# Moved value rows of a causal convolution: copied inside the chip instead of through DRAM

## The chip, the cores and the metric

The kernel runs on one core of one Trainium2 chip. The metric is the device time of one execution in microseconds (us), median of several runs. The core has five engines, each with its own instruction stream in order: TensorE (PE, matrix products), VectorE (DVE), ScalarE (ACT), GpSimd (POOL) and SyncE (SP). Data move between DRAM and the on-chip memory (128 partitions), and inside the on-chip memory too, by DMA. A DMA is issued by SP, ACT or POOL and runs on up to 16 DMA engines, beside the five engines. All numbers are float32.

## The reference, cut to what matters

One decoder layer on 256 tokens of 2048 channels. After a normalisation, one wide input projection makes q, k, v, z, two small gate inputs, a pooling input and two more gates. A causal convolution of width 4 runs over the 256 tokens of q, k and v, each channel by itself:

```python
def causal_dwconv(x, w):
    width = w.shape[0]
    seq = x.shape[1]
    xp = jnp.pad(x, ((0, 0), (width - 1, 0), (0, 0)))
    y = xp[:, 0:seq] * w[0]
    for j in range(1, width):
        y = y + xp[:, j:j + seq] * w[j]
    return y
...
qkv = jax.nn.silu(causal_dwconv(jnp.concatenate([q, k, v], axis=-1), conv_qkv_w[l]))
```

So a token's value row needs the row itself and the rows one, two and three tokens before it, each times a weight for each channel; before the first token there are zeros. The rest (the gated delta rule over the convolved q, k, v, the pooling mixer, the gates, the output projection, and a gated MLP of 5632 channels) is the same in both kernels.

## The kernel before, in words

**Work of PE.** The large products stream their weights. A tile of weights has 256 rows of the contraction and 512 columns, 512 KB, and is named `raw` when it has landed. To keep float32 accuracy it is split in two: ACT casts it to `whi` (L317, `begin`), DVE subtracts and gets `wlo` (L328), and PE does three products for each (L365 to L367, in `gemm_a`): 12 matmuls of 512 columns for each tile of weights. There are four buffers of `raw` and three pairs `whi`, `wlo`; `weights()` keeps the split two tiles ahead of the one in use. A load of `raw` is issued by SP (L223, `load_part`) as soon as the split has freed its buffer.

**Order of the input projection.** The columns are done in four groups `g` of 512 (four heads each). In each group PE projects k, q, v, the pooling input, a gate, z (with the small pooling product) and the other gate, eight tiles of weights each (`for g in range(4)`, L1095). A projection ends in a PSUM tile; `evict` (L776) scales it by the row's normaliser on ACT into the on-chip tile `e`, which has the one buffer `ev`. For k, q and v the tokens lie along the partitions: `e` is 128 partitions by 2 by 512, token `t * 128 + p` at partition `p`, half `t`.

**k and q** are turned by PE so that tokens lie along the free dimension, and their convolution is three shifted multiply-adds on DVE (`conv_silu`, L825); its result tile `y` has the tag `cy`, two buffers.

**v** stays with tokens along the partitions, where a shift by a token is a shift by a partition, which no DVE instruction does. So:
- before the projection starts, DVE sets a small tile `zr` to zero, and four DMAs issued by ACT write three zero rows ahead of each group's place in a DRAM tensor `vrow` (L768 to L774);
- after the eviction of v, SP writes `e` to `vrow` (L1122);
- in `v_moved` (L800), DVE multiplies `e` by the last tap (L802), and SP loads three copies from `vrow`, moved by one, two and three tokens (L807): each a tile `m` of 128 partitions by 2 by 512;
- in `v_conv` (L810), DVE multiplies each `m` by its tap (L816) and adds it to the sum (L817), in the order one, two, three tokens; ACT does the tanh of the silu (L820).

The homes of the three tiles `m`: the copies by one and two use the two buffers of `cy` (which k's and q's convolution results have held before), the copy by three uses the single buffer `mv` (which `zr` held at first).

**What sets the order.** Each `dma_start`, product and sum is placed on its engine's stream by a planner when the program is built; it follows the dependences, the order of the code, and a model of the durations. `tc.issue_after(x)` sets an instruction behind another. Work that is to run during the next projection is put in the list `later`, and `gemm_a` calls it when it comes to its second tile of weights (L358 to L360): `v_moved` of a group thus stands in the projection of the pooling input, just behind v's. `side()` (L368) advances the delta rule of the group by a step for every half tile of weights. In `v_conv`, the product with copy `n` is set behind the split number `splits_of[g] + n`, and three further in group 0 (L815).

The next eviction, that of the pooling input, writes the single buffer `ev` again.

Of the kernel before, what the change touches and what calls it, by code (L numbers as in the profile page):

```python
# [8 lines left out]
F32 = mybir.dt.float32  # L9
# [5 lines left out]
P = 128  # L15
S = 256
# [19 lines left out]
def kernel(  # L36
# [20 lines left out]
    nc = tc.nc  # L57
# [5 lines left out]
    dpool = ctx.enter_context(tc.tile_pool(name="dram", bufs=2, space=bass.MemoryType.DRAM))  # L63
# [5 lines left out]
    def nm(s):  # L69
        cnt[0] += 1  # L70
        return f"{s}_{cnt[0]}"
# [282 lines left out]
    def gemm_a(lh, ll, nk, steps=None, ps=None):  # L354

        ps = pm() if ps is None else ps
        for c in range(nk // 2) if steps is None else steps:
            if c == 1:  # L358
                while later:
                    later.pop(0)()  # L360
            hi, lo = weights()
            for kk in range(2):
                k = 2 * c + kk
                for t in range(2):
                    mm(ps[:, t, :], lh(k, t), hi[:, kk, :], start=(k == 0), stop=False)  # L365
                    mm(ps[:, t, :], ll(k, t), hi[:, kk, :], start=False, stop=False)  # L366
                    mm(ps[:, t, :], lh(k, t), lo[:, kk, :], start=False, stop=(k == nk - 1))  # L367
                side()  # L368
        return ps
# [65 lines left out]
    mp = mix.__enter__()  # L435
# [46 lines left out]
    def parts_x(pts):  # L482
        for k, pt in pts:
            high, low = (both(xhl, k)[:, n, :] for n in range(2))
            hi = nc.scalar.activation(high, pt, AF.Copy, scale=nmw[:, k : k + 1])
            lo = nc.vector.scalar_tensor_tensor(low, pt, nmw[:, k : k + 1], high.bitcast(F32),
                                                op0=ALU.mult, op1=ALU.subtract)
        return hi.ins, lo.ins
# [28 lines left out]
    with tc.manual_schedule(engines={mybir.EngineType.PE, mybir.EngineType.DVE, mybir.EngineType.Activation}):  # L517
# [21 lines left out]
        for c in range(4):  # L539
            if c:  # L540
                tile_k0(2 * c)
            if c < 3:
# [3 lines left out]
                last_act, last_dve = parts_x(pts[2:])  # L546
# [219 lines left out]


    SH = 3  # L768
    vrow = dpool.tile([4, SH + S, 512], F32, tag="vrow", bufs=1, name="vrow")
    zr = mp.tile([P, 2, 512], F32, tag="mv", name="zr")  # L770
    nc.vector.memset(zr[:SH, 0, :], 0.0)
    for g in range(4):
        with tc.issue_after(last_act):
            nc.scalar.dma_start(vrow[g, 0:SH, :], zr[:SH, 0, :])  # L774

    def evict(ps, by=None):  # L776

        by = rs1 if by is None else by
        e = mp.tile([P, 2, 512], F32, tag="ev", bufs=1, name=nm("ev"))
        for t in range(2):  # L780
            nc.scalar.activation(e[:, t, :], ps[:, t, :], AF.Copy, scale=by[:, t : t + 1])
        return e
# [17 lines left out]
    def v_moved(e, g, vt):  # L800

        nc.vector.tensor_tensor(vt, e, taps_of[g][3], op=ALU.mult)  # L802
        moved_of[g] = []
        splits_of[g] = len(splits)
        for j in (1, 2, 3):
            m = mp.tile([P, 2, 512], F32, name=nm("mv"), **(dict(tag="cy", bufs=2) if j < 3 else dict(tag="mv")))
            nc.sync.dma_start(m, vrow[g, SH - j : SH - j + S, :].rearrange("(t p) d -> p t d", p=P))  # L807
            moved_of[g].append(m)

    def v_conv(g, vt):  # L810
# [284 lines left out]
    for g in range(4):  # L1095
        kq = mp.tile([P, 4, 2, S], F32, tag="kq", bufs=1, name=nm("kq"))
        for kind, dst in ((1, kq[:, :, 0, :]), (0, kq[:, :, 1, :])):
            ps = ps_k0 if kind == 1 and g == 0 else gemm_a(xh, xl, KD)
            e = evict(ps)
# [19 lines left out]

            later.append(after_k)  # L1120
        e = evict(gemm_a(xh, xl, KD), rsh)
        nc.sync.dma_start(vrow[g, SH : SH + S, :].rearrange("(t p) d -> p t d", p=P), e)  # L1122
        later.append(lambda e=e, g=g, vt2=vt2: v_moved(e, g, vt2))


# [3 lines left out]
        e = evict(ps) if g == 3 else evict(ps, rsh)  # L1129
# [608 lines left out]
```

## Time and profile before

| | |
|---|---|
| time, median of 3 runs | 1537.4 us (1536.69 to 1538.38) |
| the profiled execution | 1538.56 us, of which the span from the first to the last instruction is 1536.8 us |
| granted clock of TensorE | 0.998 of full speed |
| moved rows, DMA issues | 4 writes of 512 KB, 12 loads of 512 KB, 4 zero writes of 6 KB |
| evictions of v | begin at 86.65, 263.74, 441.12 and 619.69 us |

How to read the views that follow. On the page, a line of an engine gives busy time, share of the span and number of instructions; a queue line gives packets, MB and the time of its packets as a share of 16 engines' span; q1 is SP's queue and q10 ACT's. A group of instructions gives the line of the code, the engine, the operation, the tiles it writes and reads, the count, busy time, the mean in ns, and the idle time before it with what ended it. A row of the waits says who waited for whom: total us, how often, the longest. A row of the timeline gives the start and the length in us, the engine, the line, the tiles, the count; the bracket has the idle time before it and what ended it. SPq is a DMA issued by SP. A row of the stretches gives the stretch, its length, busy time and count of PE, the weight load, DVE, ACT and POOL, then the granted clock, the busy share of the DMA engines, and GB/s. Rows of DMA issues give the count, the size of each and, where known, the median us from issue to landing.

### The profile page before, as it was taken

The page shows a single profiled execution, that of the slowest core. Times are in us where ns is not written, and L with a number is a line of the kernel's source. Part 1 is how long each engine was busy: PE and PEld are TensorE (multiplying, and loading weights), DVE is VectorE, ACT ScalarE, POOL GpSimd, SP SyncE. Part 2 cuts the span into 40 slices and gives each one's busy share as a digit, 9 for nine tenths or more (in the row PEclk, how much of TensorE's full clock was granted, in tenths as well). Part 3 has the DMA queues.
Part 4 walks back from the last instruction along what each step waited for, and adds up shares of the span by engine and source line. Part 5 has one row for each costly group of instructions (what it writes and reads, how often), then busy time and mean ns, then how long its engine had stood idle before and what let it go on. Part 6 is the DMA issues. An engine that isn't in the chain of part 4 may idle for free. (4 is left out here: it accounts for less than half of the span.)

```text
span 1536.8 us, 20233 instructions
## 1 busy us (share of the span) xinstructions
PE 1524.3 (99%) x7290; PEld 1255.4 (82%) x7290; DVE 1268.3 (83%) x1793; ACT 853.1 (56%) x1070; POOL 80.9 (5%) x105
## 2 busy tenths in 40 slices
PE   9999999999999999999999999999999999999997
PEld 8887888787878888788888888788888888888876
DVE  6788859896589858887567899999999886889896
ACT  6455446454455445454455666666666665555553
POOL 1010002000100000000000000000000011010200
PEclk9999999999999999999999999999999999999999
DMA  8776757776576766776588556656457478566662
GB/s 276 209 229 198 203 165 207 218 216 185 148 250 201 208 169 194 231 195 186 171 263 305 179 178 219 219 206 206 154 165 243 127 238 266 172 223 207 235 201 98
DMA packets 166515, 313.62 MB, mean 204 GB/s; under 512 B 19554, under 2 KB 23426, under 8 KB 166286
## 3 DMA queue, kind: packets, MB, share of 16 engines
q1 hardware_dynamic: 157280, 283.17, 59.2%
q0 software_dynamic: 7344, 27.27, 5.5%
q10 hardware_dynamic: 1790, 1.89, 0.4%
q8 instruction: 57, 0.93, 0.3%
q14 instruction: 44, 0.36, 0.1%
HBM read 303.33 MB, written 8.95 MB: 203 GB/s over the span
## 5 line engine op out<-in xcount | busy, mean ns | idle before, releaser
L317 ACT CAST whi<-raw 128x1024 fp32r<-128x1024 f32 x420 | 441.2, 1052 | 427.1 <-PE psm L366 270.0
L328 DVE TENSOR_TENSOR wlo<-raw,whi 128x1024 fp32r<-128x1024 f32 x418 | 507.7, 1220 | 146.0 <-ACT whi L317 140.2
L317 ACT CAST whi<-quad 128x1024 fp32r<-128x1024 f32 x182 | 190.5, 1053 | 136.8 <-PE psg L1418 43.5
L328 DVE TENSOR_TENSOR wlo<-quad,whi 128x1024 fp32r<-128x1024 f32 x182 | 220.0, 1219 | 30.0 <-ACT whi L317 29.4
L367 PE MATMUL psm<-wlo,xhl 128*128 128x512 f32 x432 | 169.5, 393 | 1.3 <-DVE wlo L328 1.2
L365 PE MATMUL psm<-whi,xhl 128*128 128x512 f32 x432 | 169.0, 391 | 0.0
L366 PE MATMUL psm<-whi,xhl 128*128 128x512 f32 x432 | 168.6, 390 | 0.0
L1418 PE MATMUL psg<-whi,fhl 128*128 128x512 f32 x504 | 127.2, 390 | 0.0
L1418 PEld LDWEIGHTS psg<-whi,fhl 128*128 128x128 f32 x504 | 94.5, 188 | 19.6
L367 PEld LDWEIGHTS psm<-wlo,xhl 128*128 128x128 f32 x432 | 81.1, 188 | 18.8 <-DVE wlo L328 2.2
L366 PEld LDWEIGHTS psm<-whi,xhl 128*128 128x128 f32 x432 | 81.1, 188 | 16.8
L365 PEld LDWEIGHTS psm<-whi,xhl 128*128 128x128 f32 x432 | 81.1, 188 | 16.7
L244 DVE TENSOR_TENSOR quad<-quad,quad 128x1024 f32<-128x1024 f32 x72 | 87.6, 1216 | 0.0
L1418 PE MATMUL psg<-wlo,fhl 128*128 128x512 f32 x252 | 69.9, 389 | 0.0
L1418 PE MATMUL psg<-whi,ups 128*128 128x512 f32 x216 | 58.9, 394 | 0.0
L1418 PEld LDWEIGHTS psg<-wlo,fhl 128*128 128x128 f32 x252 | 47.3, 188 | 9.9
L1403 PE MATMUL psm<-whi,hhi 128*128 128x512 f32 (+1 forms) x140 | 54.5, 389 | 0.1
L1403 PE MATMUL psm<-whi,hlo 128*128 128x512 f32 (+1 forms) x140 | 54.1, 386 | 0.0
L1403 PE MATMUL psm<-wlo,hhi 128*128 128x512 f32 (+1 forms) x140 | 54.0, 387 | 0.0
L365 PE MATMUL psm<-whi,mhi 128*128 128x512 f32 x128 | 50.8, 397 | 0.0
L367 PE MATMUL psm<-wlo,mhi 128*128 128x512 f32 x128 | 50.0, 390 | 0.0
L366 PE MATMUL psm<-whi,mlo 128*128 128x512 f32 x128 | 49.9, 390 | 0.0
(435 smaller groups left out, 2953.7 us busy)
## 6 DMA issues: line engine op xcount, KB each, us to landing
raw<-in_w_in_dram SPq DMA_DIRECT2D x224, 512.0 KB, 4.3
raw<-in_w_up_dram SPq DMA_DIRECT2D x104, 512.0 KB, 4.8
quad<-in_w_up_dram SPq DMA_DIRECT2D x72, 512.0 KB, 5.0
raw<-in_w_down_dram SPq DMA_DIRECT2D x56, 512.0 KB, 5.1
raw<-in_w_out_dram SPq DMA_DIRECT2D x32, 512.0 KB, 4.2
quad<-in_w_down_dram POOLq DMA_DIRECT2D x32, 512.0 KB, 5.3
mv<-vrow SPq DMA_DIRECT2D x12, 512.0 KB, 4.8
taps<-in_conv_qkv_w_dram SPq DMA_DIRECT2D x16, 256.0 KB, 6.6
```

Of the source, the lines that this page charges most:

```text
L244: nc.vector.tensor_tensor(out_, plus_, minus_, op=ALU.subtract)
L317: last_cast[0] = nc.scalar.copy(hi, raw).ins
L328: last_split[0] = nc.vector.tensor_tensor(lo, raw, hi.bitcast(F32), op=ALU.subtract).ins
L365: mm(ps[:, t, :], lh(k, t), hi[:, kk, :], start=(k == 0), stop=False)
L366: mm(ps[:, t, :], ll(k, t), hi[:, kk, :], start=False, stop=False)
L367: mm(ps[:, t, :], lh(k, t), lo[:, kk, :], start=False, stop=(k == nk - 1))
L1403: mm(ps[:, cs], lhs(kk), part_[:, kk, cs], start=(first and kk == 0 and n == 0), stop=(last and kk == 1 and n == 2), skip_group_check=shared)
L1418: mm(ps, lhs(kk), w[n][:, kk], start=(first and n == 0 and kk == 0 and lhs is high), stop=False, skip_group_check=True)
```

## The change

DRAM is left out of the move. The tensor `vrow`, the zero rows and the write of `e` go. Each moved tile is now made of three pieces: POOL sets its first `j` rows of half 0 to zero; a DMA issued by ACT copies the last `j` partitions of half 0 of `e` to the first `j` partitions of half 1; a DMA issued by SP copies the first `128 - j` partitions of `e`, both halves, to the partitions from `j` on. Homes: the copy by one token now uses `mv`, those by two and three use `cy`. The products and sums on them are as before.

```diff
-    vrow = dpool.tile([4, SH + S, 512], F32, tag="vrow", bufs=1, name="vrow")
-    zr = mp.tile([P, 2, 512], F32, tag="mv", name="zr")
-    nc.vector.memset(zr[:SH, 0, :], 0.0)
-    for g in range(4):
-        with tc.issue_after(last_act):
-            nc.scalar.dma_start(vrow[g, 0:SH, :], zr[:SH, 0, :])
...
         for j in (1, 2, 3):
-            m = mp.tile([P, 2, 512], F32, name=nm("mv"), **(dict(tag="cy", bufs=2) if j < 3 else dict(tag="mv")))
-            nc.sync.dma_start(m, vrow[g, SH - j : SH - j + S, :].rearrange("(t p) d -> p t d", p=P))
+            m = mp.tile([P, 2, 512], F32, name=nm("mv"), **(dict(tag="cy", bufs=2) if j > 1 else dict(tag="mv")))
+            nc.gpsimd.memset(m[0:j, 0, :], 0.0)
+            nc.scalar.dma_start(m[0:j, 1, :], e[P - j :, 0, :])
+            nc.sync.dma_start(m[j:], e[: P - j])
             moved_of[g].append(m)
...
         e = evict(gemm_a(xh, xl, KD), rsh)
-        nc.sync.dma_start(vrow[g, SH : SH + S, :].rearrange("(t p) d -> p t d", p=P), e)
         later.append(lambda e=e, g=g, vt2=vt2: v_moved(e, g, vt2))
```

## The prediction

> **What bounds the kernel now.** I read the page first (its time by engine, its DMA queues, its groups of instructions), then the waits, then the stretches around the four moves.
>
> ```profile
> span 1536.8 us, 20233 instructions
> PE 1524.3 (99%) x7290; PEld 1255.4 (82%) x7290; DVE 1268.3 (83%) x1793; ACT 853.1 (56%) x1070; POOL 80.9 (5%) x105
> ...
> q1 hardware_dynamic: 157280, 283.17, 59.2%
> ...
> q10 hardware_dynamic: 1790, 1.89, 0.4%
> ...
> L317 ACT CAST whi<-raw 128x1024 fp32r<-128x1024 f32 x420 | 441.2, 1052 | 427.1 <-PE psm L366 270.0
> ```
>
> TensorE is busy for 1524.3 of 1536.8 us: whatever the change saves elsewhere can come out only where PE stands still. The waits of the engines, and the busy time of each engine in the stretch behind a V eviction (group 0 and group 2; the first pair of numbers is the length and PE's busy time), say how little that is around the moved rows:
>
> ```profile
> DVE mv L816 <- DMA mv<-vrow: 11.2, 4, 4.5
> ```
>
> ```profile
> 86.00:112.00 26.00, 26.00 (x112) 20.86 (x112) 22.68 (x35) 12.74 (x15) 1.93 (x1) 1.00 0.83 253
> 441.00:467.00 26.00, 24.80 (x107) 19.54 (x106) 20.78 (x33) 10.52 (x13) 2.08 (x1) 1.00 0.74 241
> ```
>
> DVE waits 11.2 us in all for the moved rows, once in each of the four groups. PE feels one of the four, the longest (4.5 us): in group 2 it is busy for 24.80 of 26 us, in group 0 for all 26. So the round trip through DRAM costs this execution about 1.2 us, and a perfect change returns 1.2 us.
>
> **What is removed, and at what price.** Four writes of 512 KB (L1122), four small zero writes issued by ACT and one memset go; twelve loads of 512 KB (L807) become copies inside the chip.
>
> ```profile
> 88.72 0.47 SPq L1122 DMA_DIRECT2D vrow<-ev  x1
> 91.75 0.37 SPq L223 DMA_DIRECT2D raw<-in_w_in_dram  x1
> 94.67 0.88 SPq L807 DMA_DIRECT2D mv<-vrow  x2
> ```
>
> ```profile
> 90.51 1.22 DVE L328 TENSOR_TENSOR wlo<-raw,whi 128x1024 fp32r<-128x1024 f32 x1
> ...
> 93.31 1.23 DVE L846 SCALAR_TENSOR_TENSOR kq<-th,cy 128x1024 f32<-128x1024 f32 x1
> ...
> 96.21 1.23 DVE L328 TENSOR_TENSOR wlo<-raw,whi 128x1024 fp32r<-128x1024 f32 x1 [0.54 <-ACT whi L317]
> 99.69 1.23 DVE L816 TENSOR_TENSOR mv<-mv,taps 128x1024 f32<-128x1024 f32 x1 [2.25 <-DMA mv<-vrow]
> ```
>
> ```profile
> 103.18 0.39 PE L365 MATMUL psm<-whi,xhl 128*128 128x512 f32 x1
> ...
> 105.90 0.39 PE L365 MATMUL psm<-whi,xhl 128*128 128x512 f32 x1
> ```
>
> ```profile
> DMA to landing us min/median/max: 4.3/4.8/5.0
> ```
>
> In group 0 SP issues the write at 88.72 and the loads only from 94.67, when the write has landed. Straight copies can go at about 88.7, 6.0 us sooner. Were each as quick as the loads (4.8 us), DVE's 2.25 us stall would go; the next thing late is nothing on PE. This part is worth 0 to -1.2 us over the whole run, and I take -1.2.
>
> **What is added: how many DMA engines serve a copy.** The loads land 128 partitions. The copies land 127, 126 and 125 (`m[j:]`). The profile has no such transfer on SP's queue, but ACT's queue q10 has some with odd counts, and its packets can be counted from the list of issues:
>
> ```profile
> psb<-in_pool_scale_dram ACTq DMA_DIRECT2D x4, 256.0 KB
> ...
> out_dram<-xt ACTq DMA_DIRECT2D x2, 256.0 KB
> ...
> cqrows<-in_conv_qkv_w_dram ACTq DMA_DIRECT2D x1, 96.0 KB, 2.9
> cfrows<-in_conv_ffn_w_dram ACTq DMA_DIRECT2D x1, 66.0 KB
> gwb<-in_gdn_norm_w_dram ACTq DMA_DIRECT2D x1, 64.0 KB, 3.8
> vrow<-zr ACTq DMA_DIRECT2D x4, 6.0 KB
> vrows<-in_conv_ffn_b_dram ACTq DMA_DIRECT2D x1, 22.0 KB
> nmrows<-in_norm_mix_w_dram ACTq DMA_DIRECT2D x1, 8.0 KB
> alb<-in_a_log_dram ACTq DMA_DIRECT2D x1, 8.0 KB
> dtb<-in_dt_bias_dram ACTq DMA_DIRECT2D x1, 8.0 KB
> vrows<-in_norm_ffn_w_dram ACTq DMA_DIRECT2D x1, 8.0 KB, 3.4
> ```
>
> By the shapes in the code these 18 transfers consist of 512 + 256 + 192 + 132 + 128 + 12 + 44 + 16 + 128 + 128 + 16 = 1564 contiguous pieces. The queue shows 1790 packets, 226 more. If every transfer ended with one packet on each of 16 engines there would be 288 more. The 62 that are missing are what the odd shapes leave out if a transfer runs on the largest number of engines, 16 at most, that divides its rows: 3 rows on 3 engines (4 times 13 missing), 66 and 44 rows on 11 each (twice 5): 52 + 10 = 62. SP's queue, where all counts are multiples of 16, fits with 16 each. So I take the rule that the rows give: 127 rows are prime and go on **one** engine, 126 on 14, 125 on 5.
>
> The Trainium skill says the same of transfers issued from SP and ACT, with 127 partitions on one engine as an example (page "DMA: Bandwidth & Descriptors", section "Why a DMA increments its semaphore by 16 and not by 1"); the 226 agree, but no run so far shows 127 rows.
>
> **The price of one engine.** I take the time of a packet from a stretch in which the engines were nearly full, 30.61 to 32.95 us:
>
> ```profile
> q1 hardware_dynamic: 397, 0.78, 95.1%
> ```
>
> 0.951 x 16 x 2340 ns / 397 = 89.7 ns for a packet of 2 KB, so 179 ns for a row of 4 KB. (All of q1 on the page gives 92.6 ns.) The copy by one row: 127 x 179 = 22.8 us on one engine. By two: 126/14 = 9 rows, 1.6 us. By three: 125/5 = 25 rows, 4.5 us. A weight load: 256 packets over 16 engines, 1.4 us on each. An engine that all three use is held for 28.9 us, and it serves a sixteenth of every weight load behind them on SP's queue.
>
> **What waits for it, in group 0.** A tile of weights feeds 12 matmuls, 2.72 us (103.18 to 105.90, both first matmuls of a tile). Four raw buffers: the split that ends at 91.73 frees the one for the tile that PE begins at 105.90, and its load goes out at 91.75, behind the copies. It has to be there by 105.90 - 1.05 (cast) - 1.22 (split) = 103.6. A load of 4.8 us is 7.1 us early; that is the cover. Of those 4.8 us 1.4 are packets, so 3.4 are start and queue. With the copies out at 88.7 the first lands at 88.7 + 3.4 + 22.8 = 114.9. The load behind it and behind the copy by two lands at 114.9 + 1.6 + 1.4 = 117.9, its tile is ready at 120.2, and PE stands for 14.3 us. The copy by three waits for its new home until the q convolution has been read (93.31 + 1.23 = 94.5), as the loads did, so it may stand ahead of the next load: that one lands at 117.9 + 4.5 + 1.4 = 123.8 and is ready at 126.1, 3.2 us after PE wants it. Upper reading 17.5 us. The start may overlap with what is in flight, which takes up to 3.4 us off: lower reading 10.9 us.
>
> DVE gives nearly the same by its own way: the product L816 stands behind the split of 96.21, and the splits behind it wait for the first copy until 114.9. The split of that same tile would end at about 114.9 + 1.2 + 1.2 = 117.3, against PE's 105.90: 11.4 us. The two waits run side by side, and the longer counts. I take **15 us a group**, inside 10.9 to 17.5. In the other groups the product may stand three splits earlier (the code sets it behind a split three tiles sooner there), and PE would run dry sooner but also wait for the same landing. Four groups: 60 us.
>
> **The small pieces** (12 memsets on POOL, 12 ACT copies of 2 to 6 KB).
>
> ```profile
> L774 ACTq DMA_DIRECT2D vrow<-zr x4: 238/265/283, 28.2 to 30.2; - x4
> ```
>
> Three issues of 0.27 us are 0.8 us of ACT, busy for 12.74 of 26 us in that stretch; POOL has one instruction there, 1.93 us. On ACT the third waits for the same home as SP's copy by three (94.5); a cast behind it could lose 0 to 1.4 us. Three memsets on POOL, each at most as long as that instruction, are at most 5.8 us, in an engine that is idle for 24. I take 0; if POOL or ACT held the copies back as well, the bound is 3 us a group, 12 in all. The next eviction reuses `ev` and now waits on ACT until the copies have read it, at 114.9 + 1.6 + 4.5 = 121.0; PE ends that projection at 120.2 + 2.7 = 122.9, so nothing is added.
>
> **The sum.** -1.2 + 60 = +59 us, rounded: 1596 us span against 1536.8. The profiled execution took 1538.56 us beside a median of 1537.4 (1536.69 to 1538.38), so I put it on the median: 1596.5.
>
> **The rivals.**
> - *The copies are spread over all 16 engines after all.* Then each lands in about 4.8 us, DVE's four waits go, and PE gets back its 1.2 us: 1536.2 us, not slower. It decides at one point: a first copy that lands in under about 12 us from its issue (4.8 plus the 7.1 of cover) stalls no load. For it: all twelve loads of 128 rows landed in 4.3 to 5.0. Against it: the 62 missing packets. The same section of the Trainium skill tells of direct copies issued from GpSimd that put 127 rows on 16 engines; by that 1536.2 would come out, but these go from SP. Chance 0.08.
> - *The cover is larger than I count*: two more weight loads slip ahead of the copies, so that the first delayed tile is needed 2 x 2.72 us later, and the start overlaps wholly. 15 - 5.4 - 3.4 = 6.2 us a group, +24 in all: 1561 us. For it: SP's order is planned anew, and SP issued one load between the write and the loads of rows. Against it: a raw buffer comes free only every 2.72 us, and the copies need nothing that is later than 88.7. Chance 0.05.
> - *The waits chain*: memset, ACT's piece and SP's copy one behind the other, or one engine slower still when it reads and writes inside the chip. A first copy 1.75 times as long, 40 us for 22.8, adds 17 a group: +128, about 1665 us. Chance 0.07.
> - The forecast, 0.80.
>
> The range has my readings and bounds: 4 x 8.2 - 1.2 (10.9 less one load slipped ahead, 2.7) = +31, 1568, to 4 x 20.5 + 12 - 1.2 = +93, 1630 (17.5, and about one tile, 3 us, more where the product stands three splits earlier; 12 for the small pieces). It leaves out 0.20. A measurement of this kernel tells about 0.2%, 3 us, from no change. Even spread gives "same" nearly always: same 0.06, faster 0.02, slower 0.92.
>
> **What would show it.** Right: `mv<-ev` copies that land 20 us or more after their issue; DVE waiting some 15 us a group for them at the product; weight loads in the same 25 us that land in 15 to 25 us; PE busy for some 11 of the 26 us behind each V eviction, and as full as before elsewhere. On q1 four groups lose 4 x 272 packets each (the write and three loads, 256 + 16) and get 128 + 140 + 130 (rows and one packet for each engine): 157280 - 2760 = 154520, where an even spread over 16 would leave 154632. Wrong: copies that land in 5 us, or PE full in those stretches. If they are slow but PE stands for under 8 us a group, the cover was undercounted; if PE loses time outside the four stretches, a wait on ACT or POOL that I put at 0 is the cause.

## The result and the profile after

The changed kernel takes 1626.93 us (median of 4 runs, 1624.64 to 1628.39) beside 1537.55 us for the kernel before: a ratio of 1.058, 95% interval 1.0567 to 1.0593. The forecast was 1596.5 us, range 1568 to 1630. The loss has the sign, the place and the cause that were forecast, and is half as large again: +89.4 us against +59.

The page after; its lines answer to those of the page before (span, time by engine, queues):

```profile
span 1625.3 us, 20278 instructions
PE 1537.4 (95%) x7290; PEld 1260.8 (78%) x7290; DVE 1267.2 (78%) x1792; ACT 853.0 (52%) x1070; POOL 84.1 (5%) x117
...
q1 hardware_dynamic: 154520, 280.98, 55.8%
```

DVE and ACT do the same work as before. The span is 88.5 us longer, and PE's busy time 13.1 us: the rest, 75.4 us, is PE standing still. SP's queue has 154520 packets, which is the number worked out for copies on 1, 14 and 5 engines; an even spread would have left 154632.

The waits after, with total, times and longest:

```profile
ACT whi L317 <- DMA raw<-in_w_in_dram: 99.2, 14, 22.8
DVE mv L812 <- DMA mv<-ev: 94.6, 7, 22.0
...
PE psm L367 <- DVE wlo L328: 58.3, 11, 18.3
```

The second row was 11.2 us in 4 times before, and the first was small:

```profile
ACT whi L317 <- DMA raw<-in_w_in_dram: 7.4, 4, 2.5
```

ACT waits for weight loads, DVE for the moved rows, PE for DVE's splits.

The 26 us behind the four V evictions (from 87, 282, 480 and 679 us):

```profile
87.00:113.00 26.00, 19.46 (x83) 15.03 (x81) 10.57 (x14) 6.69 (x8) 0.52 (x1) 0.97 0.45 131
282.00:308.00 26.00, 15.61 (x66) 11.93 (x64) 5.91 (x5) 6.44 (x8) 0.52 (x1) 0.90 0.49 137
480.00:506.00 26.00, 10.93 (x49) 8.72 (x47) 5.44 (x8) 5.79 (x7) 0.00 (x0) 0.77 0.32 97
679.00:705.00 26.00, 11.01 (x49) 8.79 (x47) 5.63 (x7) 5.60 (x8) 0.52 (x1) 0.81 0.33 98
```

Where PE was full, it now works for 11 to 19 of 26 us, and the DMA engines are busy for a third to a half (share next to last) instead of about three quarters and more. For part of the time one of them works alone: from 500 to 505 us SP's queue has 31 packets of 4 KB, one row each, and they take 6.2% of 16 engines' time, which is one engine of 16.

Group 0 in order of time, first SP's issues, then DVE, then ACT:

```profile
84.22 5.23 SPq L223 DMA_DIRECT2D raw<-in_w_in_dram  x3
89.96 2.48 SPq L803 DMA_DIRECT2D mv<-ev  x2
93.04 12.32 SPq L223 DMA_DIRECT2D raw<-in_w_in_dram  x2
```

```profile
97.20 1.23 DVE L328 TENSOR_TENSOR wlo<-raw,whi 128x1024 fp32r<-128x1024 f32 x1 [0.79 <-ACT whi L317]
117.34 1.23 DVE L812 TENSOR_TENSOR mv<-mv,taps 128x1024 f32<-128x1024 f32 x1 [18.92 <-DMA mv<-ev]
```

```profile
119.99 1.04 ACT L317 CAST whi<-raw 128x1024 fp32r<-128x1024 f32 x1 [22.82 <-DMA raw<-in_w_in_dram]
```

The first copy goes out at 89.96, and DVE can use it at 117.34: 27.4 us. In groups 1, 2 and 3 the same distance is 26.1, 25.2 and 24.4 us. The weight load issued at 93.04, behind the copies, is there for the cast at 119.99, 27 us later; such a load took 4.3 us before (median).

The holes of PE that are longer than 2 us, all of them (five rows of PE's timeline; the bracket is the hole):

```profile
121.09 0.79 PE L365 MATMUL psm<-whi,xhl 128*128 128x512 f32 x1 [14.63 <-ACT whi L317]
...
313.13 0.79 PE L367 MATMUL psm<-wlo,xhl2b 128*128 128x512 f32 x1 [15.53 <-DVE wlo L328]
...
320.27 0.80 PE L367 MATMUL psm<-wlo,xhl 128*128 128x512 f32 x1 [2.60 <-DVE wlo L328]
...
509.28 0.80 PE L367 MATMUL psm<-wlo,xhl2a 128*128 128x512 f32 x1 [18.34 <-DVE wlo L328]
...
707.88 0.79 PE L367 MATMUL psm<-wlo,xhl2a 128*128 128x512 f32 x1 [17.88 <-DVE wlo L328]
```

Together 69.0 us, one large hole in each group. In group 0 a late weight load ends the large hole, in the others the splits behind the product that waited.

### The profile page after: what moved, and what is told of

It is laid out like the page before. It is cut to its first block, busy times and chain, and to the rows that moved or that the text cites. A ratio compares the mean times of both kernels' runs of the same rounds, so it can differ in the third digit from the quotient of the medians.

```text
span 1625.3 us, 20278 instructions
## 1 busy us (share of the span) xinstructions
PE 1537.4 (95%) x7290; PEld 1260.8 (78%) x7290; DVE 1267.2 (78%) x1792; ACT 853.0 (52%) x1070; POOL 84.1 (5%) x117
## 3 DMA queue, kind: packets, MB, share of 16 engines
q1 hardware_dynamic: 154520, 280.98, 55.8%
q0 software_dynamic: 7344, 27.27, 5.1%
q10 hardware_dynamic: 1934, 1.91, 0.4%
## 5 line engine op out<-in xcount | busy, mean ns | idle before, releaser
L365 PE MATMUL psm<-whi,xhl 128*128 128x512 f32 x432 | 170.5, 395 | 14.6 <-ACT whi L317 14.6
L812 DVE TENSOR_TENSOR mv<-mv,taps 128x1024 f32<-128x1024 f32 x12 | 14.7, 1223 | 94.6 <-DMA mv<-ev 94.6
L367 PE MATMUL psm<-wlo,xhl2a 128*128 128x512 f32 x108 | 44.6, 413 | 36.2 <-DVE wlo L328 36.2
L367 PE MATMUL psm<-wlo,xhl2b 128*128 128x512 f32 x108 | 43.7, 405 | 16.3 <-DVE wlo L328 16.3
```

Source lines behind the costliest of these rows:

```text
L812: nc.vector.tensor_tensor(m, m, taps_of[g][j], op=ALU.mult)
```

## The experiments

**The theory:** a DMA with 127 rows runs on one DMA engine and one with 125 rows on five; DVE's product waits for the copy, and the weight loads behind it on SP's queue wait for their sixteenth. **Rivals:** the transfer inside the chip is slow whatever its shape; the small pieces on POOL and ACT are what waits; the exchange of homes. Ratios are to the kernel before, with 95% intervals.

| kernel | median, us | ratio |
|---|---|---|
| the change | 1626.93 | 1.0580 [1.0567, 1.0593] |
| large copies cut into 112 + (16 - j) rows | 1543.6 | 1.0042 [1.0028, 1.0056] |
| through DRAM, 127, 126, 125 rows | 1637.18 | 1.0653 [1.0637, 1.0668] |
| only the 127 rows cut | 1555.15 | 1.0115 [1.0097, 1.0133] |
| only the 126 and 125 rows cut | 1616.76 | 1.0512 [1.0493, 1.0530] |
| homes put back | 1621.08 | 1.0537 [1.0516, 1.0558] |
| products later | 1621.77 | 1.0541 [1.0525, 1.0557] |
| large copies issued by ACT | 1632.65 | 1.0615 [1.0599, 1.0631] |
| large copies issued by GpSimd | 1545.34 | 1.0049 [1.0034, 1.0064] |
| cut, homes put back | 1542.72 | 1.0030 [1.0018, 1.0042] |
| cut, products 3 tiles later | 1535.73 | 0.9985 [0.9976, 0.9993] |
| cut, both | 1536.39 | 0.9990 [0.9981, 0.9998] |
| kernel before, products 3 tiles later | 1535.84 | 0.9989 [0.9980, 0.9998] |

**1. The number of rows, and nothing else.**

```diff
-            nc.sync.dma_start(m[j:], e[: P - j])
+            nc.sync.dma_start(m[16:], e[16 - j : P - j])
+            nc.sync.dma_start(m[j:16], e[: 16 - j])
```

> The changed kernel with each large copy cut in two: 112 rows (16 to 127 of the moved tile) and the 16 - j rows above them, so that 112 rows can go over 16 engines and 15, 14 or 13 rows over as many. Zeros, ACT's small pieces, homes and the in-chip path stay. One engine for 127 rows is the cause: 1536 to 1539 us, DVE waits for moved rows under 5 us in all, PE without the four holes of 14 to 18 us. The in-chip transfer as such is slow, or the small pieces on POOL and ACT are what waits: 1610 to 1630 us.

Measured 1543.6 us: 83 of the 89 us are gone. The same bytes go by the same path, with the same small pieces. SP's queue has 154800 packets: 280 more than in the change, as the rule gives for 112 rows on 16 engines and 15, 14 and 13 rows on as many. PE's busy time in the four stretches (from 86, 264, 441 and 619 us) comes back:

```profile
86.00:112.00 26.00, 26.00 (x113) 20.87 (x112) 24.86 (x40) 12.79 (x15) 2.96 (x3) 1.00 0.87 252
264.00:290.00 26.00, 25.72 (x108) 19.99 (x108) 22.23 (x35) 10.38 (x12) 2.04 (x3) 1.00 0.81 219
441.00:467.00 26.00, 26.00 (x113) 20.88 (x112) 23.55 (x38) 11.69 (x13) 2.04 (x3) 1.00 0.79 234
619.00:645.00 26.00, 26.00 (x113) 20.87 (x112) 20.79 (x28) 12.48 (x15) 0.56 (x2) 1.00 0.75 215
```

But 1536 to 1539 had been expected, and DVE still waits 10.8 us for the moved rows, where under 5 had been expected. The 6 us that are left are taken up in experiment 6.

**2. The same row counts through DRAM.** The kernel before, its loads cut as the change cuts its copies:

```diff
-            nc.sync.dma_start(m, vrow[g, SH - j : SH - j + S, :].rearrange("(t p) d -> p t d", p=P))
+            rows = vrow[g, SH - j : SH - j + S, :].rearrange("(t p) d -> p t d", p=P)
+            nc.scalar.dma_start(m[0:j], rows[0:j])
+            nc.sync.dma_start(m[j:], rows[j:])
```

> The kernel before (by way of DRAM, its homes), but each load of 128 moved rows cut as the changed kernel cuts its copies: 127, 126 or 125 rows by SP and the first 1, 2 or 3 by ACT. No memset, nothing copied inside the chip. One engine for 127 rows is the cause: the loss is here too, 1600 to 1640 us. The in-chip transfer is what is slow: 1537 to 1542 us.

Measured 1637.18 us, a larger loss than the change's: the write to DRAM comes first, and the loads are not much quicker for it (in group 0 the 127 rows are asked for at 94.15 us, not at 89.96, and DVE can use them 26.0 us later). There is no memset here, no copy inside the chip and no exchange of homes. PE's waits are the same kind:

```profile
PE psm L367 <- DVE wlo L328: 86.7, 6, 23.2
```

So neither the path nor the pieces that the change added make the bulk of the loss. The row count does, in both directions: cut it and the loss goes (1), bring it into the kernel before and the loss comes (2).

**3. Which of the three copies.** In the first kernel only the copy by one token is cut (`if j == 1`), in the second only the two others (`if j > 1`):

```diff
-            nc.sync.dma_start(m[j:], e[: P - j])
+            if j == 1:
+                nc.sync.dma_start(m[16:], e[16 - j : P - j])
+                nc.sync.dma_start(m[j:16], e[: 16 - j])
+            else:
+                nc.sync.dma_start(m[j:], e[: P - j])
```

> The changed kernel with only the copy by one token cut into 112 and 15 rows; those by two (126 rows, 14 engines) and three (125 rows, 5 engines) stay whole. If the 127 rows on one engine make the loss: engines that serve all are held for about 1.6 + 4.5 + 1.6 us, within or near the cover of 7 us: 1537 to 1550 us. If any copy that isn't on 16 engines does it, or the three together: 1580 us or more.

> The reverse: the copy by one token whole (127 rows), those by two and three cut into 112 and 14 or 13 rows. If the 127 rows make the loss: 1595 to 1627 us, four holes of PE of 12 to 17 us, each followed by some us at a lower granted clock. If the copies by two and three make it: under 1560 us.

Measured 1555.15 and 1616.76 us. Both speak for the 127 rows: the second lies in the range given for them (1595 to 1627), and the first is far below the 1580 of the other reading, though 5 us above its range (1537 to 1550). The whole copies by two and three still cost something (PE's largest holes are 4.1 and 2.9 us). Above the kernel with all three cut (1543.6), the 127 rows alone cost 73.2 us and the two others 11.5 us; the sum, 84.7, is near the 83.3 of the change. So the costs of the copies nearly add up.

**4. The homes.**

```diff
-... if j > 1 else dict(tag="mv")))
+... if j < 3 else dict(tag="mv")))
```

> The changed kernel with the homes of the three tiles put back: the copies by one and two in the two buffers of cy, the copy by three in mv. One engine for 127 rows is the cause: 1615 to 1635 us, as with the exchange. The exchange of homes makes a part of the loss (in groups 2 and 3 of the changed kernel the copy by three goes out 30 us after the first): 1600 us or less.

Measured 1621.08 us: 6 us of 89. The exchange isn't the cause of the loss.

**5. Two waits side by side.** First the products are asked for later, so that DVE no longer waits at the first of them; then the copies leave SP's queue for ACT's, so that the weight loads no longer stand behind them; then GpSimd issues them.

```diff
-            with tc.issue_after(splits[splits_of[g] + n + (3 if g == 0 else 0)]):
+            with tc.issue_after(splits[splits_of[g] + n + 10]):
```

> The changed kernel with the three products of the moved rows set behind splits about seven (group 0) to ten (the others) tiles later, so that DVE asks for the copies some 20 to 27 us later and isn't held at the first of them. The weight loads still stand behind the copies in SP's queue. Loads and DVE are held side by side, each long enough: 1595 to 1630 us, and it is now ACT that waits for the loads. DVE's wait alone makes the loss: 1540 to 1555 us.

Measured 1621.77 us. DVE waits for no moved rows any more, and PE's waits are now for ACT's casts, which wait for the loads:

```profile
PE psm L365 <- ACT whi L317: 50.7, 5, 14.5
PE psg L1007 <- DVE T L983: 8.4, 2, 7.7
```

The loads alone hold PE for 50.7 us, 12.7 a group. (The later products also make the end of group 3 late, 7.7 us in the second row, so the total says less than the first row.)

```diff
-            nc.sync.dma_start(m[j:], e[: P - j])
+            nc.scalar.dma_start(m[j:], e[: P - j])
```

> The changed kernel with the large copies issued by ACT, so that the weight loads on SP's queue don't stand behind them; DVE still waits for the same rows. The wait of DVE is long enough by itself (11 us a group by the prediction's reckoning), and ACT may stand in its issues as SP did for 8 us: 1590 to 1640 us. The order in SP's queue makes the loss: 1540 to 1560 us.

Measured 1632.65 us, and not for the reason alone that was under test. ACT's timeline in group 0:

```profile
88.12 0.71 ACTq L803 DMA_DIRECT2D mv<-ev  x1
88.86 10.17 ACTq L802 DMA_DIRECT2D mv<-ev  x1
99.06 0.87 ACTq L803 DMA_DIRECT2D mv<-ev  x1
100.03 1.99 ACT L317 CAST whi<-raw 128x1024 fp32r<-128x1024 f32 x2 [12.09 <-issue]
```

Behind the 127 rows, ACT stands for 10.17 us in the issue of two rows, and its casts with it. PE then waits 28.2 us in all for casts and 40.5 us for splits, 32.0 of these in three holes behind the late product (groups 1 to 3). So this run doesn't isolate DVE's wait; it shows that moving the copy to another queue moves the stand to that queue's issuer.

```diff
-            nc.sync.dma_start(m[j:], e[: P - j])
+            nc.gpsimd.dma_start(m[j:], e[: P - j])
```

> The changed kernel with the large copies issued by GpSimd. If the number of engines goes by the rows whoever issues: 1600 to 1640 us. If GpSimd's copies of 127 rows go over all 16 engines (the Trainium skill's exception): 1537 to 1550 us, and a first copy that lands in under 10 us.

Measured 1545.34 us. The landings of the twelve copies, the same 127, 126 and 125 rows:

```profile
DMA to landing us min/median/max: 4.8/8.0/9.9
```

GpSimd's queue has 1728 packets more than in the change (9072 beside 7344), near the 1704 of an even spread over 16 engines. With 1, 14 and 5 engines it would have been 1592, which is what ACT's queue got when ACT issued the copies (3526 beside 1934). So the row count matters by who issues. The Trainium skill (page "DMA: Bandwidth & Descriptors", section "Why a DMA increments its semaphore by 16 and not by 1") tells of this exception for GpSimd; the landing of at most 9.9 us agrees with it.

**6. The last 6 us.** The planner follows a model of durations. It moved the products forward and the q convolution back, presumably because its model has the rows there sooner than by way of DRAM. In group 3 of the kernel with cut copies DVE then has (three rows of its timeline):

```profile
623.38 1.23 DVE L813 TENSOR_TENSOR mv<-mv,taps 128x1024 f32<-128x1024 f32 x1 [0.38 <-DMA mv<-ev]
...
632.51 1.22 DVE L843 SCALAR_TENSOR_TENSOR kq<-th,cy 128x1024 f32<-128x1024 f32 x1
...
640.69 1.22 DVE L813 TENSOR_TENSOR mv<-mv,taps 128x1024 f32<-128x1024 f32 x1 [4.69 <-DMA mv<-ev]
```

The same step of the q convolution before:

```profile
622.12 1.22 DVE L846 SCALAR_TENSOR_TENSOR kq<-th,cy 128x1024 f32<-128x1024 f32 x1
```

The last step of the q convolution starts at 632.51 instead of 622.12, and the last product waits 4.69 us. PE feels it later, in holes of 1.74 and 0.97 us at 673 and 683 us, which wait for splits. Three kernels: homes back, products three tiles later in groups 1 to 3, both.

```diff
-            with tc.issue_after(splits[splits_of[g] + n + (3 if g == 0 else 0)]):
+            with tc.issue_after(splits[splits_of[g] + n + 3]):
```

> The copies cut in two (112 and 16 - j rows) with the homes of the kernel before (one and two in cy, three in mv). The 6 us that the cut copies still lose come from the exchange of homes (in group 3 POOL and the copy by three wait 14 us for a home, the longest hole of PE follows): 1536 to 1540 us. They come from the order of DVE, which is planned anew in any case: 1541 to 1546 us.

> The cut copies with the exchanged homes, and the three products set behind splits three tiles later in groups 1 to 3, as group 0 has it from the start. DVE's early stand at the first product is what is left: 1536 to 1540 us. The homes: 1541 to 1546 us as before.

> The cut copies with both: homes of the kernel before, and products three tiles later. If either of the two makes the 6 us: 1536 to 1540 us, at best 1.2 us under the kernel before. If neither (the small pieces on ACT and POOL, or the contention of the copies): 1541 to 1546 us.

Measured 1542.72, 1535.73 and 1536.39 us. The place of the products is what was left; the homes do little by themselves. With the products later PE waits for no such split any more. The kernel with cut copies and later products is 0.15% under the kernel before (interval 0.07 to 0.24%). Is that the change's gain? The same line in the kernel before:

> The kernel before, by way of DRAM, with nothing changed but the three products set three tiles later in groups 1 to 3. If the cut copies inside the chip are needed for the 2 us under the kernel before: 1537 to 1538.5 us. If the later products alone make them, by taking away the 1.2 us hole of group 2 and DVE's four waits: 1535 to 1536.5 us.

Measured 1535.84 us, ratio 0.9989 [0.9980, 0.9998]. PE is full in the two stretches that had been 25.86 and 24.80 us:

```profile
264.00:290.00 26.00, 26.00 (x109) 20.20 (x109) 23.74 (x43) 10.80 (x12) 1.01 (x1) 1.00 0.73 234
441.00:467.00 26.00, 26.00 (x109) 20.21 (x108) 23.04 (x42) 10.32 (x12) 1.01 (x1) 1.00 0.73 239
```

The intervals overlap. So the round trip through DRAM can be hidden by asking for the rows three tiles later, and what a good copy inside the chip adds beyond that is too small to be seen.

## Why the prediction was right, point by point, and where its size was off

- **One engine for 127 rows: right.** It was inferred from 62 missing packets on ACT's queue; SP's queue has exactly the forecast 154520, and experiments 1 and 2 turn the loss off and on by the row count alone.
- **The price of the copy: right as a sum.** 26.2 us from issue to landing (3.4 and 22.8) was reckoned; 24.4 to 27.4 us passed until DVE could use it. The two parts are off in opposite ways, which is luck: the 31 rows from 500 to 505 us give 0.062 x 16 x 5000 ns / 31 = 160 ns a row instead of 179, so 127 rows are an estimated 20.3 us, and 4 to 7 us are left for the start and the rest.
- **Two waits side by side: right.** Loads alone (products later) hold PE for 12.7 us a group, where 10.9 to 17.5 was reckoned. That DVE's wait alone is long enough wasn't isolated. In the changed kernel DVE waits for the moved rows for 94.6 us, 23.7 a group, more than the some 15 that the forecast named as a sign.
- **15 us a group: too small.** The holes are 14.6, 18.1 (in two parts), 18.3 and 17.9 us, 69.0 for 60. Group 0, the one that was worked out, came as reckoned (14.3). In the others the product does stand earlier, PE runs dry sooner, and the landing comes hardly sooner. With the products later the holes of groups 1 to 3 are 14.5, 11.3 and 11.0 us, so the early product is worth some 4 to 7 us of each. The working said this, but gave it a price (about 3 us a group) only in the upper end of the range, not in the sum.
- **A term that was missing: the clock after a hole.** PE's busy time is 13.1 us longer with the same 7290 matmuls. The stretch right after group 0's hole, and two matmuls inside and two behind the slow part:

```profile
121.00:126.00 5.00, 4.87 (x12) 3.44 (x13) 4.93 (x8) 1.08 (x2) 1.06 (x1) 0.57 0.43 124
```

```profile
123.36 0.63 PE L366 MATMUL psm<-whi,xhl 128*128 128x512 f32 x1
123.79 0.63 PE L367 MATMUL psm<-wlo,xhl 128*128 128x512 f32 x1
...
125.86 0.39 PE L367 MATMUL psm<-wlo,xhl 128*128 128x512 f32 x1
126.08 0.39 PE L365 MATMUL psm<-whi,xhl 128*128 128x512 f32 x1
```

  The granted clock is 0.57 there. A matmul starts every 0.43 us instead of every 0.22: the ten from 121.09 on take 4.3 us instead of 2.3. The same follows the other four holes; the 46 slow matmuls together lose some 9 to 10 of the 13.1 us, and the rest is open. The Trainium skill has it (page "TensorE: Matmul & The Clock Gate", section "Part 1: The HAM clock gate"): half the clock after an idle time of some 3.4 us, until PE has been busy about as long again. The trace agrees for the way back, with 4.3 us behind the first hole and 3 to 5 us behind the others. It doesn't for the idle time: the hole of 2.60 us was followed by half the clock too (0.50 from 321 to 323 us), and so was one of 2.90 us in the kernel with only the 127 rows cut (a mean of 0.71 from 470.6 to 473 us).
- **-1.2 us for the round trip: wrong.** The cut copies show what the change is worth when its copies are quick: +6 us. The forecast took the order of DVE as given and only removed a wait from it. The planner made a new order, which cost more than the wait, and the wait didn't go: DVE stood for 10.8 us in 5 times instead of 11.2 in 4. In the change, PE's idle time outside the five holes grew by 75.4 - 69.0 = 6.4 us, about as much. PE stands still for 5.1 us of the stretch from 730 to 830 us, with holes of 1.64 and 0.95 us that wait for splits, as the holes of 1.74 and 0.97 us in the kernel with cut copies do. So the 6 us are likely the same; no run of the change with its slow copies shows it.
- **The small pieces and the next eviction at nothing: right as far as tested.** With 112 rows the small pieces are all still there, and PE is all but full in the four stretches. In the changed kernel no eviction waits for the copies; in the one with the products ten tiles later one waits 8.6 us. The forecast would have put time lost outside the four stretches down to ACT or POOL; in the kernel with cut copies experiment 6 finds the place of the products instead.

The sum as it came out: 69.0 in holes, 13.1 of busy time, 6.4 elsewhere, 88.5 us of span; the forecast had 60, 0 and -1.2. That 1626.93 still lies in the range is in part luck. The upper end holds 12 us for the small pieces, which didn't need them; without these it would have been about 1618. The slow clock, for which the range had no term, took their place.

## What to carry to other kernels

Before a transfer is moved or trimmed, look at the row count of its outermost dimension: on the queue of SP or ACT one row fewer than 128 turned 16 engines into one here, and what then stands still is all that is queued behind, not only who asked for the rows. Cut such a copy into a part with a multiple of 16 rows and a small rest. When a hole of PE is priced, add the time for which the clock stays down behind it, and when a planner sets the order, don't count a removed wait as a gain before the new order is seen.

## What the runs showed of the hardware that had not been expected

**An issuer stands behind its own backlog.** The copies' issues on SP in the changed kernel (shortest, median, longest in ns):

```profile
L803 SPq DMA_DIRECT2D mv<-ev x12: 662/1214/8442, 90.0 to 714.4; - x12
```

Before:

```profile
L807 SPq DMA_DIRECT2D mv<-vrow x12: 366/462/471, 94.7 to 625.6; - x12
```

The 8.4 us are the copy by two right behind the 127 rows (group 2); with the copies on ACT's queue an issue of two rows took 10.17 us. From 486 to 490 us, within the 8.4 us, the DMA engines' share is 0.06, one engine of 16, which is at its 127 rows while the others are free. Why the issue stands isn't shown.

**Half the clock after a hole** costs some 1.5 to 2.5 us for each, as above, and makes a stall of 15 us one of 17.
